# Two DRAM stretches with 64 KB rows in place of three stretches: x * y with a tanh GELU, one core

## The chip, the cores and the metric

One core of a Trainium2 chip. The time is the device time of one execution in microseconds (us); the kernel before takes 119.73 us (median of three runs, 119.72 to 119.74). Every later measurement has its own runs of the kernel before beside it on the same chip. A run would count as slow if it were over 1.5% above the fastest of its kernel. A **ratio** below is the mean time of one kernel's fast runs over the mean of the other's fast runs of the same rounds, with a 95% interval; it is therefore not quite the ratio of the medians that stand beside it.

## The reference

```python
batch, dim = 1024, 4096            # x, y: float32, 16 MiB each
z = x * y
out = 0.5 * z * (1 + tanh(sqrt(2 / pi) * (z + 0.044715 * z**3)))
```

It is elementwise, so any cut of the flat array into rows for the 128 partitions will do, as long as x, y and out are cut alike. 33.55 MB are read and 16.78 MB written.

## The kernel before

Each partition holds all of its 32,768 columns of x (128 KB); y gets room for 20,440 columns and is brought in by three loads. DRAM is cut into three stretches, each contiguous, with rows of 5 KB, 64 KB and 60,416 bytes for each partition (the code is shortened):

```python
PIECES = [(0, 1280), (1280, 17664), (17664, 32768)]            # x loads, and how DRAM is cut
Y_LOADS = [(1280, 17664, 4056), (17664, 32768, 0), (0, 1280, 15104)]   # columns, place in ys
Y_FREE = [0, 3, 4]                                             # multiplies done before that y load
STEPS = [[4096] * 4, [2048] * 7 + [768], [1280]]
STORES = [(1280, 17664), (17664, 32768), (0, 1280)]

def columns(t, a, b):                     # DRAM rows of columns a:b, contiguous stretch by stretch
    flat = t.flatten_outer_dims().rearrange("r c -> (r c)")
    pa, pb = next(q for q in PIECES if q[0] <= a and b <= q[1])
    return flat[P * pa : P * pb].rearrange("(p c) -> p c", p=P)[:, a - pa : b - pa]

_hoist(nc, [load_x(0).ins, load_x(1).ins])       # ahead of the start barriers, on SP's queue
load_y(0)
load_x(2)
for i in range(1, len(Y_LOADS)):
    if Y_FREE[i]:
        nc.sync.wait_ge(sem_mul, Y_FREE[i])
    load_y(i)
# ... for each load and each step of it: VectorE multiplies, ScalarE applies GELU, both in place in xs
for i, (a, b) in enumerate(STORES):
    if i == 0:
        nc.sync.wait_ge(sem_y[-2], 16)           # the second y load has landed
    nc.sync.wait_ge(sem_act, done[b])
    nc.sync.dma_start(out=columns(out, a, b), in_=xs[:, a:b]).then_inc(sem_o[i], 16)
```

All nine transfers go through one queue, in the order x (5 KB), x (64 KB), y (64 KB), x (60,416), y (60,416), y (5 KB), then the stores (64 KB, 60,416, 5 KB). Each of the 16 DMA engines moves eight rows of every transfer, one packet a row, with one ending packet of 4 bytes behind them: 16 x 9 x (8 + 1) = 1296 packets, as the trace has.

## Time and profile before

| | before |
|---|---|
| time, median | 119.73 us |
| span of the profiled run | 118.3 us |
| VectorE / ScalarE busy | 35.2 / 31.0 us |
| packets of the one queue | 1296, 98.8% of 16 engines' span |
| all loads landed (last 5 KB y packets) | 78.82 to 79.17 us |
| first store done, by engine | 98.30 to 98.49 us |
| second store issued | 96.33 us |
| last packet | 117.93 us |

The last four rows come from the trace's record of packets and instructions. (In the views DVE is VectorE, ACT is ScalarE, and SP is the engine that issues the transfers; an engine with a q, as SPq, is its sequencer.) To read it: the packets of the trace before move at 27.1 bytes per ns and engine for rows of 64 KB and of 60,416 bytes (medians 2420 and 2229 ns) and at 26.1 for rows of 5 KB (196 ns), so while every engine's packets follow without a gap, its time here goes with its bytes; what matters are the places where a transfer could reach an engine too late, and packets that take longer than others of their size.

### The profile page before, as it was taken

Reading aid. Unit: us, or ns where it says so; the run is one execution under the profiler, and the core shown is the slowest. Engines: PE = TensorE matmul, PEld = TensorE weight load, DVE = VectorE, ACT = ScalarE, POOL = GpSimd, SP = SyncE. Lnnn points to the kernel's source line nnn. Section 1 sums busy time; section 2 is a strip of 40 time slices with the busy share of each in tenths; the row PEclk is TensorE's granted clock in tenths of the full one; section 3 lists DMA queues with packets and bytes.
Section 4 is the critical chain, followed back from the end, with each engine's and each line's share of the span. In section 5 each row is a group of like instructions: output and inputs, shape, how many; then the busy total and the mean of one; then the engine's idle time right before and its main releaser. Section 6 shows DMA issues by size and latency. Waiting matters only on the chain.

```text
span 118.3 us, 82 instructions
## 1 busy us (share of the span) xinstructions
DVE 35.2 (30%) x13; ACT 31.0 (26%) x14; POOL 0.2 (0%) x4
## 2 busy tenths in 40 slices
DVE  0000000000000069999920000059999940000000
ACT  3000000000000001977974000007998990000000
POOL 0000000000000000000000000000000000000000
DMA  9988899889988897797797797798899888977975
GB/s 375 556 355 355 355 643 421 355 355 421 643 355 355 355 654 327 327 654 327 327 654 327 327 654 327 327 576 355 355 576 487 355 355 368 613 327 327 654 327 222
DMA packets 1296, 50.33 MB, mean 425 GB/s; under 512 B 144, under 2 KB 144, under 8 KB 528
## 3 DMA queue, kind: packets, MB, share of 16 engines
q1 hardware_dynamic: 1296, 50.33, 98.8%
HBM read 33.55 MB, written 16.78 MB: 425 GB/s over the span
## 4 chain that ended last, share of the span: by engine, by line
DMA 53%; DVE 24%; ACT 3%; issue 1%; DVEq 0%
DMA ys<-in_y_dram 53%; DVE xs L96 24%; ACT xs L104 3%; DVEq L93 0%
## 5 line engine op out<-in xcount | busy, mean ns | idle before, releaser
L96 DVE TENSOR_TENSOR xs<-xs,ys 128x2048 f32<-128x2048 f32 (+3 forms) x13 | 35.2, 2778 | 60.7 <-DMA ys<-in_y_dram 60.7
L104 ACT ACTIVATE xs<-xs 128x2048 f32<-128x2048 f32 (+3 forms) x13 | 29.7, 2301 | 64.5 <-DVE xs L96 64.5
L104 ACT ACT_TABLE_LOAD x1 | 1.3, 1283 | 1.9 <-PEq L59 1.9
L134 POOL MEMSET const-bfloat16-1.0<- 128x1 bf16 x1 | 0.1, 102 | 0.0
L134 POOL MEMSET const-uint8-127<- 128x1 uint8 x1 | 0.1, 102 | 0.0
L134 POOL MEMSET const-float32-0.0<- 128x1 f32 x1 | 0.1, 99 | 0.2 <-issue 0.2
L134 POOL MEMSET const-float32-1.0<- 128x1 f32 x1 | 0.1, 99 | 0.0
## 6 DMA issues: line engine op xcount, KB each, us to landing
xs<-in_x_dram SPq DMA_DIRECT2D x1, 7552.0 KB, 57.9
ys<-in_y_dram SPq DMA_DIRECT2D x1, 7552.0 KB, 22.5
out_dram<-xs SPq DMA_DIRECT2D x1, 7552.0 KB, 20.4
xs<-in_x_dram SPq DMA_DIRECT2D x1, 640.0 KB, 3.6
ys<-in_y_dram SPq DMA_DIRECT2D x1, 640.0 KB, 19.7
out_dram<-xs SPq DMA_DIRECT2D x1, 640.0 KB, 20.8
xs<-in_x_dram SPq DMA_DIRECT2D x1, 22.6
ys<-in_y_dram SPq DMA_DIRECT2D x1, 40.4
```

The costliest lines, as they stand in the source:

```text
L96: nc.vector.tensor_mul(out=xs[:, c : c + w], in0=xs[:, c : c + w], in1=ys[:, r + c - a : r + c - a + w],).then_inc(sem_mul, 1)
L104: nc.scalar.activation(out=xs[:, c : c + w], in_=xs[:, c : c + w], func=GELU).then_inc(sem_act, 1)
L134: nc = _bacc.Bacc("TRN2", target_bir_lowering=False, num_devices=1)
```

## The change

Two stretches with 64 KB rows. The 5 KB that are first of x and last of y become the tail of the second stretch's rows, so that one store of full 64 KB rows replaces the stores of 60,416-byte and 5 KB rows. Since that store needs the tail's columns as well, their step moves from the end to the second place.

```diff
@@ -11,14 +11,20 @@
 
 
 
-PIECES = [(0, 1280), (1280, 17664), (17664, 32768)]
+PIECES = [(0, 16384), (16384, 32768)]
+X_LOADS = [(31488, 32768), (0, 16384), (16384, 31488)]
 
-Y_LOADS = [(1280, 17664, 4056), (17664, 32768, 0), (0, 1280, 15104)]
+Y_LOADS = [(0, 16384, 4056), (16384, 31488, 0), (31488, 32768, 15104)]
 
 Y_FREE = [0, 3, 4]
 
-STEPS = [[4096] * 4, [2048] * 7 + [768], [1280]]
-STORES = [(1280, 17664), (17664, 32768), (0, 1280)]
+STEPS = [
+    *((0, c, 4096) for c in range(0, 16384, 4096)),
+    (1, 16384, 2048),
+    (2, 31488, 1280),
+    *((1, c, min(2048, 31488 - c)) for c in range(18432, 31488, 2048)),
+]
+STORES = PIECES
 Y_BUF = 20440
 
 
@@ -60,14 +66,14 @@
 
     xs = nc.alloc_sbuf_tensor("xs", [P, PIECES[-1][1]], F32).ap()
     ys = nc.alloc_sbuf_tensor("ys", [P, Y_BUF], F32).ap()
-    sem_x = [nc.alloc_semaphore(f"sem_x{i}") for i in range(len(PIECES))]
+    sem_x = [nc.alloc_semaphore(f"sem_x{i}") for i in range(len(X_LOADS))]
     sem_y = [nc.alloc_semaphore(f"sem_y{i}") for i in range(len(Y_LOADS))]
     sem_mul = nc.alloc_semaphore("sem_mul")
     sem_act = nc.alloc_semaphore("sem_act")
     sem_o = [nc.alloc_semaphore(f"sem_o{i}") for i in range(len(STORES))]
 
     def load_x(i):
-        a, b = PIECES[i]
+        a, b = X_LOADS[i]
         return nc.sync.dma_start(out=xs[:, a:b], in_=columns(x, a, b)).then_inc(sem_x[i], 16)
 
     def load_y(i):
@@ -84,32 +90,27 @@
             nc.sync.wait_ge(sem_mul, Y_FREE[i])
         load_y(i)
 
-    n = 0
-    done = {}
-    for i, (a, b, r) in enumerate(Y_LOADS):
-        for j, (xa, xb) in enumerate(PIECES):
-            if xa <= a < xb:
-                nc.vector.wait_ge(sem_x[j], 16)
-        nc.vector.wait_ge(sem_y[i], 16)
-        c = a
-        for w in STEPS[i]:
-            nc.vector.tensor_mul(
-                out=xs[:, c : c + w],
-                in0=xs[:, c : c + w],
-                in1=ys[:, r + c - a : r + c - a + w],
-            ).then_inc(sem_mul, 1)
-            n += 1
-            done[c + w] = n
-            nc.scalar.wait_ge(sem_mul, n)
-            nc.scalar.activation(
-                out=xs[:, c : c + w], in_=xs[:, c : c + w], func=GELU
-            ).then_inc(sem_act, 1)
-            c += w
+    seen = set()
+    for n, (i, c, w) in enumerate(STEPS, 1):
+        a, b, r = Y_LOADS[i]
+        if i not in seen:
+            seen.add(i)
+            nc.vector.wait_ge(sem_x[X_LOADS.index((a, b))], 16)
+            nc.vector.wait_ge(sem_y[i], 16)
+        nc.vector.tensor_mul(
+            out=xs[:, c : c + w],
+            in0=xs[:, c : c + w],
+            in1=ys[:, r + c - a : r + c - a + w],
+        ).then_inc(sem_mul, 1)
+        nc.scalar.wait_ge(sem_mul, n)
+        nc.scalar.activation(
+            out=xs[:, c : c + w], in_=xs[:, c : c + w], func=GELU
+        ).then_inc(sem_act, 1)
 
     for i, (a, b) in enumerate(STORES):
         if i == 0:
             nc.sync.wait_ge(sem_y[-2], 16)
-        nc.sync.wait_ge(sem_act, done[b])
+        nc.sync.wait_ge(sem_act, max(n for n, (_, c, _) in enumerate(STEPS, 1) if a <= c < b))
         nc.sync.dma_start(out=columns(out, a, b), in_=xs[:, a:b]).then_inc(sem_o[i], 16)
     for i in range(len(STORES) - 1):
         nc.sync.wait_ge(sem_o[i], 16)
```

## The prediction

Where the recorded texts are marked as cut, here and among the experiments, they said of the hardware what no trace or run of this case shows.

> **What bounds the kernel now.** I began with the page: the span, the busy times and the row of DMA shares.
>
> ```profile
> span 118.3 us, 82 instructions
> DVE 35.2 (30%) x13; ACT 31.0 (26%) x14; POOL 0.2 (0%) x4
> DMA  9988899889988897797797797798899888977975
> q1 hardware_dynamic: 1296, 50.33, 98.8%
> ```
>
> Both compute engines are idle for two thirds of the span, while the packets of one queue fill 98.8% of the 16 DMA engines' time. The dips in the DMA digits are not idle time: a packet of up to 64 KB is booked where it ends or starts, which is also why the GB/s row swings between 327 and 654. So the second thing I read was the trace's record of every DMA packet (start, length, size). Counting only the 1152 data packets: the first starts at 1.04 us, the last ends at 117.92 us, and in between all 16 engines have a packet in flight except in the first and last fraction of a microsecond. There are 384 packets each of 65,536, 60,416 and 5,120 bytes, with medians of 2420, 2229 and 196 ns. That is 27.1, 27.1 and 26.1 bytes per ns for one engine: a 5 KB row is only 4% less efficient than a 64 KB row. The other 144 packets carry 4 bytes, 9 ns each: one for each engine at the end of each of the nine transfers.
>
> The page's chain of waits gives 53% to the y loads and 24% to VectorE, and ends in ScalarE; it does not follow the queue, and here that matters. The waits of the DMA-issuing engine show the end better:
>
> ```profile
> SPq L115 <- DMA out_dram<-xs: 18.9, 1, 18.9
> SPq L113 <- ACT xs L104: 18.7, 2, 17.9
> SPq L113 <- DMA ys<-in_y_dram: 14.5, 1, 14.5
> SPq L119 <- SPq L119: 1.4, 1, 1.4
> ```
>
> The two waits on ScalarE (18.7 us together) are those ahead of the second and third store. [...]The timeline at that place tells how close it is:
>
> ```profile
> 93.66 3.80 ACT L104 ACTIVATE xs<-xs 128x2048 f32<-128x2048 f32 x3 [0.29 <-DVE xs L96]
> 94.41 1.49 DVE L96 TENSOR_TENSOR xs<-xs,ys 128x1280 f32<-128x1280 f32 x1
> 96.33 1.49 SPq L113 DMA_DIRECT2D out_dram<-xs  x2
> ```
>
> The second store is issued at 96.33 us, when the 768-column activation is done; the third at 97.49 us, when the 1280-column one is done. The packet records say that the engines finish the first store between 98.30 and 98.49 us. So the second store has 2.0 us to spare, and the third, queued behind 18 us of the second, has 18 us.
>
> [...]16 engines at 27.1 bytes per ns are 433 here[...]. The change gives the 5 KB transfers a pitch of 64 KB; [...]the 64 KB rows already lie at that pitch, and move at the same 27.1 as the 60,416-byte rows.[...]
>
> **The loads.** The same six transfers of the same row sizes are issued in the same order under the same waits; only where the 5 KB and 60,416-byte rows lie in DRAM changes. Packets before and after: 24 small, 24 of 60,416 and 24 of 65,536 bytes for each engine become 16, 16 and 32. I take 0 for the loads, with 0 to 0.2 us for the first transfer: its first packets now take 194 to 732 ns[...], and 128 rows spread over 8 MB could be colder than 640 KB in one piece.
>
> **The stores.** For each engine eight rows of 60,416 and eight of 5,120 bytes become eight of 65,536. Packets of one size follow each other a few ns sooner than their length, so by lengths: before, 8 x (2229 + 200) = 19,432 ns (the 5 KB store packets average about 200) plus one 9 ns semaphore packet more; after, 8 x 2418 = 19,344 ns. That saves about 0.09 us, 0.1 with the semaphore. One store issue (0.33 us) also goes, but it ran beside the stream and bounded nothing. So the whole of the intended gain is about 0.1 us, 0.1%.
>
> **What the order of the steps does.** The second store now needs all thirteen activations, not twelve. VectorE's total is unchanged: it starts at 78.12, and the 1280 step moves from last to second place. Its y has landed by then (the y wait passed at 79.62, and the second multiply starts at 80.33), so no new wait. From the rows by form, and the start of each instruction in the trace:
>
> ```profile
> L96 DVE TENSOR_TENSOR xs<-xs,ys 128x2048 f32<-128x2048 f32 x7 | 15.5, 2286 | 18.2 <-DMA ys<-in_y_dram 18.2
> ...
> L96 DVE TENSOR_TENSOR xs<-xs,ys 128x1280 f32<-128x1280 f32 x1 | 1.5, 1486 | 0.0
> ...
> L96 DVE TENSOR_TENSOR xs<-xs,ys 128x768 f32<-128x768 f32 x1 | 1.0, 951 | 0.0
> ```
>
> The 768 multiply starts at 93.54 before; with the 1280 step ahead of it, 1.49 - 0.08 = 1.40 us later, at 94.95. The last 2048 multiply therefore ends at 95.03. Its activation starts about 0.03 us later and takes 1.91 us: done at 96.97. The 768 activation overlaps it by 0.09 us and takes 0.83: done at 97.70. SP issues 0.025 us after an activation, as at 96.33 and 97.49: the second store goes out at about **97.73 us**, 1.40 us later than before, since a 768 step of ScalarE behind a 2048 step now closes the line.
>
> **What that does to the queue.** How soon does a store move data after its issue? The first store gives it: issued at 78.043, and four engines that had finished the last y packets early started its first packets at 78.887, 78.899, 78.920 and 78.951, waiting some 50 to 65 ns for them. So the earliest engine needs 0.84 us, and the sixteenth not more than 1.13 (it started at 79.178, when its own y work ended). Applied to 97.73 this gives first packets between 98.57 and at most 98.87. The engines are free at 98.30 to 98.50. So there is a **bubble of about 0.3 us** that the kernel before does not have, since its second store has a 2 us margin.
>
> **The sum.** The last engine starts at about 98.72 (between 98.62 and 98.87), moves 8 x 2415 = 19,320 ns by the pitch of packets, with 0.03 for the somewhat slower first ones and the semaphore: the last packet at about 98.72 + 19.35 = 118.07, against 117.93. The wait at the end passes 0.36 us after it, as now (118.287 against 117.926). Span about 118.45, so +0.15; I add 0.05 for the colder first load. Time: 119.73 + 0.2 = **119.93 us**, +0.17%: gain 0.1, bubble -0.3, load -0.05 or so, rounded.
>
> **The rivals.**
> 1. *The stream is what counts, and the bubble does not appear.* Fewer packets and stores then give about -0.1 us: 119.6. For it: the stream fills 98.8%. Against it: the margin of the second store sinks from 2.0 us to about 0.6, less than the 0.84 us that an issue takes. It would need ScalarE or VectorE 0.3 us faster than their rows.
> 2. *The 64 KB pitch slows the small loads.* [...]if a 5 KB packet took twice as long, two loads of eight packets for each engine would add 2 x 8 x 0.196 = 3.1 us: 122.9, slower by 2.6%. A fifth more would add 0.6. [...]Against: the 64 KB rows of this trace lie at this pitch, are walked by the engines nearly in step, and lose nothing.
> 3. *The 5 KB y load is late for its new place.* It is now needed second, not last. It lands at 79.18 and the wait passes at 79.62, while VectorE is busy until 80.4: 0.7 us of slack. If rival 2 held, this slack would go first, and each further delay would push the second store by as much, to the bubble's account.
>
> **Range and chances.** The bubble's size is set by two differences of a few tenths (97.73 and 0.84 to 1.13 against 98.30 to 98.50), and each can be off by 0.1 to 0.15; the cold load by 0.1; another chip by some hundredths. So 119.7 to 120.25 should hold it 8 times in 10. A gain of 2% would need 2.4 us, more than all idle time in the queue: chance 0.005. A loss of 2% needs rival 2 nearly in full: 0.03. Within 2%: 0.965.
>
> **What would show it.** Right, if the profile after has 1280 packets; two stores, the second issued near 97.7; a gap of 0.2 to 0.5 us at each DMA engine between the stores, where the kernel before has none; the loads' end still near 79.2. Wrong, if the 5 KB packets exceed 196 ns in the second small load, if the second store is issued before 97.4, or if its first packets follow the first store's without a gap.

## More of the kernel before

The page's list of transfers gives for each kind the KB and the us from issue to landing:

```profile
out_dram<-xs SPq DMA_DIRECT2D x1, 7552.0 KB, 20.4
xs<-in_x_dram SPq DMA_DIRECT2D x1, 640.0 KB, 3.6
ys<-in_y_dram SPq DMA_DIRECT2D x1, 640.0 KB, 19.7
out_dram<-xs SPq DMA_DIRECT2D x1, 640.0 KB, 20.8
```

The three small transfers (640 KB) take most of that time waiting in the queue (eight packets of 196 to 199 ns on average are 1.6 us for an engine, of 19.7 and 20.8), except the first x load, which nothing precedes: 3.6 us for 640 KB.

## The result, and the profile after

The changed kernel takes **120.44 us** (median of six runs, 120.38 to 120.69) against 119.75 (119.72 to 119.93): ratio 1.0061 [1.0048, 1.0074]. It is 0.6% slower, within the 2% that counts as the same, but above the range that was forecast. Measured once more, beside other runs of the kernel before: 120.58 against 119.81, ratio 1.0056 [1.0041, 1.0071].

First the page of the changed kernel: span, busy times, DMA shares, queue.

```profile
span 119.1 us, 80 instructions
DVE 35.2 (30%) x13; ACT 31.0 (26%) x14; POOL 0.2 (0%) x4
DMA  6998899888988898797797797798899888988888
q1 hardware_dynamic: 1152, 50.33, 98.6%
```

Compute is the same to a tenth. The queue has 1152 packets, 144 fewer. (The prediction's last paragraph said 1280: it took off the 16 ending packets of the store that goes and forgot its 128 rows, though its own count of 64 row packets for each engine, with one ending packet for each of eight transfers, gives 16 x 72 = 1152.) Next the waits of the DMA-issuing engine, the four longest, and the timeline around the issue of the second store:

```profile
SPq L81 <- DVE xs L100: 57.3, 2, 53.4
SPq L120 <- SPq L120: 19.5, 1, 19.5
SPq L114 <- ACT xs L106: 19.3, 1, 19.3
SPq L114 <- DMA ys<-in_y_dram: 14.5, 1, 14.5
```

```profile
93.42 1.91 ACT L106 ACTIVATE xs<-xs 128x2048 f32<-128x2048 f32 x1 [0.29 <-DVE xs L100]
95.62 2.64 ACT L106 ACTIVATE xs<-xs 128x2048 f32<-128x2048 f32 x2 [0.29 <-DVE xs L100]
98.28 0.34 SPq L114 DMA_DIRECT2D out_dram<-xs  x1
```

The first line is the wait for room in y, ahead of the later y loads. There is one wait of a store on ScalarE in line 114, where the kernel before had two in its line 113; the pair of activations that starts at 95.62 (2048 and 768 columns) ends at 98.26, and the store goes out at 98.28. Before, it was 96.33. Third, the rows of the multiplies by form, and the list of transfers:

```profile
L100 DVE TENSOR_TENSOR xs<-xs,ys 128x2048 f32<-128x2048 f32 x7 | 15.6, 2284 | 18.3 <-DMA ys<-in_y_dram 18.3
...
L100 DVE TENSOR_TENSOR xs<-xs,ys 128x1280 f32<-128x1280 f32 x1 | 1.5, 1485 | 0.0
...
L100 DVE TENSOR_TENSOR xs<-xs,ys 128x768 f32<-128x768 f32 x1 | 0.9, 949 | 0.0
```

```profile
xs<-in_x_dram SPq DMA_DIRECT2D x1, 640.0 KB, 4.2
ys<-in_y_dram SPq DMA_DIRECT2D x1, 640.0 KB, 19.7
out_dram<-xs SPq DMA_DIRECT2D x2, 20.8
```

The steps are as long as before. The first x load took 4.2 us where it took 3.6; the small y load, in the middle of the stream, is unchanged at 19.7.

The packet records say where 0.75 us of the profiled stream went (last packet at 118.67 us, against 117.93):

| from the packet records | before | after |
|---|---|---|
| first x load, 5 KB packets: longest | 732 ns | 1165 ns |
| first x load: landed, last engine | 3.20 us | 3.83 us |
| third x load: excess of its packets, per engine | 0.02 us | 0.17 us |
| all loads landed, last engine | 79.17 us | 79.68 us |
| first store done, mean of the engines | 98.38 us | 98.91 us |
| gap of an engine between first and second store, mean | 0.006 us | 0.274 us |
| first store done to last store done, means | 19.42 us | 19.67 us |

**Excess** here and below is the sum, over a transfer's packets, of the time beyond what packets of that size usually take (196, 2229 and 2418 ns), divided by 16 engines: roughly what a transfer loses per engine. The **gap** counts from the start of an engine's last ending packet, which takes 9 ns in the traces, so 0.006 us means no pause. So 0.5 us were lost by the end of the loads and 0.25 us in the stage of the stores.

### The profile page after: what moved, and what is told of

Read it like the earlier page. It is cut to its first block, busy times and chain, and to the rows that moved or that the text cites. A ratio compares the mean times of both kernels' runs of the same rounds, so it can differ in the third digit from the quotient of the medians.

```text
span 119.1 us, 80 instructions
## 1 busy us (share of the span) xinstructions
DVE 35.2 (30%) x13; ACT 31.0 (26%) x14; POOL 0.2 (0%) x4
## 2 busy tenths in 40 slices
DMA packets 1152, 50.33 MB, mean 423 GB/s; under 512 B 128, under 2 KB 128, under 8 KB 384
## 3 DMA queue, kind: packets, MB, share of 16 engines
q1 hardware_dynamic: 1152, 50.33, 98.6%
## 4 chain that ended last, share of the span: by engine, by line
DMA 53%; DVE 25%; ACT 2%; issue 1%; DVEq 0%
DMA ys<-in_y_dram 53%; DVE xs L100 25%; ACT xs L106 2%; DVEq L99 0%
## 6 DMA issues: line engine op xcount, KB each, us to landing
ys<-in_y_dram SPq DMA_DIRECT2D x1, 640.0 KB, 19.7
```

## The experiments

Theories at the outset. **T1:** the bubble between the stores costs about 0.3 us. **T2:** the first load is slow because its 128 short rows now lie spread over DRAM, and that costs the rest. Rivals: the gap or the slow first load cost nothing by themselves; it is the power-of-two pitch and not the spread; it is the new loop. Some kernels read wrong addresses on purpose, so their results are wrong in the columns concerned; this is said at each. Loads only read x, so such a probe moves the same bytes.

### First group, on one chip (119.80 us for the kernel before)

**e1_early_store**: the changed kernel with its last steps cut small, so that less of ScalarE's work stands behind VectorE's last multiply.

```diff
-    *((1, c, min(2048, 31488 - c)) for c in range(18432, 31488, 2048)),
+    # (1, start, columns), contiguous from 18432 on, of these sizes:
+    # 2048, 2048, 2048, 1536, 1536, 1280, 1024, 768, 768
```

> Only the step sizes at the end differ from the changed kernel: 1536, 1536, 1280, 1024, 768, 768 in place of three steps of 2048 and one of 768. From the rows of the changed kernel (VectorE 1.04 ns a column plus 71 ns a step, ScalarE 0.83 ns a column plus about 100 ns a step) the last activation should end at 97.46 us instead of 98.26, so the second store goes out 0.8 us earlier and its packets are ready before the engines finish the first store (98.84 to 99.01). Theory (the loss is 0.5 us of slow first load plus a bubble of about 0.25 us between the stores): the bubble goes, the rest stays: about 0.25 us faster than the changed kernel's 120.44, so 120.15 to 120.25, and no gap between the stores in the packet records. Rival (the first load alone made the loss, a gap between the stores is just how two stores of 64 KB rows follow each other): still 120.4.

Measured: 120.03 us, ratio 1.0030 [1.0014, 1.0046], against 1.0056 and 1.0061 for the changed kernel. Its timeline before the second store:

```profile
95.44 0.95 DVE L108 TENSOR_TENSOR xs<-xs,ys 128x768 f32<-128x768 f32 x1
95.67 1.59 ACT L114 ACTIVATE xs<-xs 128x768 f32<-128x768 f32 x2
97.29 0.34 SPq L122 DMA_DIRECT2D out_dram<-xs  x1
```

The store goes out at 97.29 us in place of 98.28, and every engine starts its packets 6 ns after the start of its last ending packet: the gap is gone, and with it 0.31 to 0.37 us (1.0056 to 1.0061 less 1.0030 is 0.26 to 0.31% of 119.8; each ratio is uncertain by about 0.2 us, so the packet records are the sharper evidence: 19.34 us from the first store's end to the last's in place of 19.67). That is T1, and about half of the loss. The other half stays.

**e2_contiguous** and **e3_pitch59k**: the changed kernel, its first load reading another part of x on purpose: 640 KB in one piece from the middle of x, or rows 60,416 bytes apart.

```diff
+        if i == 0:   # e2; wrong numbers on purpose
+            src = flat[P * 16384 : P * 16384 + P * 1280].rearrange("(p c) -> p c", p=P)[:, :1280]
+        if i == 0:   # e3; wrong numbers on purpose
+            src = flat[P * 16384 : P * 16384 + P * 15104].rearrange("(p c) -> p c", p=P)[:, :1280]
```

> The changed kernel, but the first small load reads its 128 rows of 5 KB from one contiguous stretch of 640 KB in x (wrong numbers in those 1280 columns on purpose). Theory (rows spread over 8 MB make the first packets slow): the first load's last packet ends near 3.2 us as before the change instead of 3.83, everything behind moves up by about 0.5 us, time about 119.95. Rival (the start of the changed kernel is slower for another reason, such as the instruction's form or the place in the tensor's second half): no change, 120.4.

> As the contiguous probe (wrong on purpose in those 1280 columns), but the 128 rows of 5 KB lie 60,416 bytes apart, over 7.7 MB, so not at a power of two. If it is the spread over many places not touched before, nothing comes back: first load done near 3.8 us, 120.4. If it is the power-of-two pitch[...], it is as the contiguous probe: done near 3.2 us, 119.95.

Measured: e2 120.36 us, ratio 1.0046 [1.0034, 1.0058]; e3 120.22 us, 1.0038 [1.0025, 1.0051]. Neither came out as one of its alternatives in full: in e2 the load landed as early as T2 said but the time was the rival's, and e3 lies between its two. In e2 the first load did land early (last engine 3.08 us, excess 0.20), but the long rows of the next loads were slower (excess 0.25 for the second x load and 0.18 for the first y load, against 0.02 and 0.01 in the changed kernel), and the total hardly moved. In e3 the first load has an excess of 0.50, less than the 0.78 of the changed kernel, so a power of two is not needed for a slow first load. Neither the clean T2 nor the pitch rival stands after this pair; it took the mirror experiments below, in a kernel without bubble.

**e4_long_first**: the changed kernel, the 64 KB rows of x loaded first.

```diff
-X_LOADS = [(31488, 32768), (0, 16384), (16384, 31488)]
+X_LOADS = [(0, 16384), (31488, 32768), (16384, 31488)]
```

> The changed kernel with the first two x loads in the other order: the 64 KB rows first, the 5 KB rows of x behind them. If the slow packets belong to the start (each engine's first reads are late, whatever is read), the 64 KB rows take the delay: first packets some 0.3 to 0.9 us over 2420 ns, and the 5 KB packets behind them 196 ns each; the end of the x loads near 22.9 us or a little less, time 120.2 to 120.4. If they belong to the 5 KB rows at their pitch, these are slow in second place too, and the long rows lose 0.1 us or so: 5 KB packets well over 196 ns, time 120.4. If a long first packet hides the delay of the reads behind it, up to 0.5 us comes back: 119.95.

Measured: 120.42 us, ratio 1.0051 [1.0039, 1.0063], about as the changed kernel. The long first packets now take up to 3238 ns (excess 0.64 us), and the same 5 KB rows in second place 202 ns on average. So in this run it is not the short rows at their pitch that are slow but the load that is read first.

### Second group: one part alone, in the kernel before (119.76 us for it)

**g1_before_spread**: the kernel before, its first load reading 5 KB rows 64 KB apart.

```diff
+        if i == 0:   # wrong numbers on purpose
+            src = flat[P * 16384 : P * 32768].rearrange("(p c) -> p c", p=P)[:, 15104:]
```

> The kernel before, only that its first small x load reads 128 rows of 5 KB that lie 64 KB apart, as the changed kernel's does (wrong numbers in those 1280 columns on purpose). So far a contiguous first load in the changed kernel gave 0.2 us of excess packet time per engine instead of 0.5 to 0.78, but the total hardly moved. Theory (spread rows cost at the start and this costs time): first load done at 3.5 to 3.8 us instead of 3.20, time 0.3 to 0.5 us over the kernel before: 120.1 to 120.3. Rival (what the spread first load loses, the long rows behind it win back, as the kernel before pays 0.18 us there): 119.8 to 119.9.

Measured: 120.05 us, ratio 1.0020 [1.0006, 1.0033], some 0.24 us. Its first small load takes nearly as long as in the changed kernel (KB, us from issue to landing):

```profile
xs<-in_x_dram SPq DMA_DIRECT2D x1, 640.0 KB, 4.1
```

The excess is 0.69 us in the first load, and 0.01 in the second, which costs 0.18 in the kernel before. So part of what the slow first load loses is won back at once, as the rival said, but a part of 0.24 us stays (0.07 to 0.40 us by the interval).

**g2_before_order**: the kernel before with the changed order of steps (and the changed kernel's loop for it), layout and stores as they were.

```diff
-STEPS = [[4096] * 4, [2048] * 7 + [768], [1280]]
+STEPS = [
+    *((0, c, 4096) for c in range(1280, 17664, 4096)),
+    (1, 17664, 2048),
+    (2, 0, 1280),
+    *((1, c, min(2048, 32768 - c)) for c in range(19712, 32768, 2048)),
+]
```

> The kernel before, only that the 1280-column step comes second in the last stretch and the 768-column step last, as in the changed kernel; layout, loads and three stores as before. Theory of the bubble: the second store is issued at 97.7 instead of 96.33 us, its packets start 0.2 to 0.3 us after the engines are free, time 0.2 to 0.3 us over the kernel before: 119.95 to 120.1. Rival (the gap costs nothing by itself): 119.8.

Measured: 120.09 us, ratio 1.0026 [1.0014, 1.0039], 0.31 us.

```profile
95.38 2.64 ACT L108 ACTIVATE xs<-xs 128x2048 f32<-128x2048 f32 x2 [0.29 <-DVE xs L101]
98.05 0.82 SPq L116 DMA_DIRECT2D out_dram<-xs  x2
```

The second store is issued at 98.05 in place of 96.33; the engines are free from 98.59 to 98.85 on, and get its packets after a mean gap of 0.273 us. From the first store's end to the last's it takes 19.75 us in place of 19.42. The bubble is shown from both sides: taken out of the changed kernel and put into the kernel before, 0.33 us each time in this stage.

**f3_three_pieces** and **h1_warm**: the early-store version, once with the tail as a third contiguous stretch at the end of DRAM with its own store (first line), once with a tiny load ahead of all (the rest).

```diff
+PIECES = [(0, 16384), (16384, 31488), (31488, 32768)]     # f3
+    warm = nc.sync.dma_start(                             # h1
+        out=ys[:, 0:128], in_=flat[: P * 128].rearrange("(p c) -> p c", p=P)
+    ).then_inc(sem_w, 16)
+    _hoist(nc, [warm.ins, load_x(0).ins, load_x(1).ins])
```

> The changed kernel with the early second store (smaller last steps, 120.03 in its own run), and the 5 KB columns as a third contiguous stretch at the end of DRAM with a store of their own, so long rows of 60,416 bytes are contiguous again and the first load is too. If the whole loss lies in the spread small rows and the bubble, this is level with the kernel before: 119.75 to 119.85. If the place (end of the tensor in place of its start) or the code of the loop matters, it stays at 120.0.

> The early-store version of the changed kernel (120.03 in its own run) with one more load ahead of all: 128 rows of 512 bytes, contiguous, into a part of the y buffer not yet in use. If the slow first packets are the engines' own start (any first read), the tiny load takes the delay and the 5 KB rows behind it move at 196 ns: first small load's excess under 0.1 us per engine, total 119.8 or less. If it is the spread of the rows over DRAM, the 5 KB packets are still slow behind the tiny load (excess 0.4 us or more) and the total is 120.0 to 120.2.

Measured: f3 120.04 us, ratio 1.0020 [1.0007, 1.0032], not level with the kernel before; its first load is contiguous but at another place, and has an excess of 0.41 us. h1 121.32 us, ratio 1.0124 [1.0111, 1.0138]: the 5 KB rows behind the tiny load are as slow as without it (excess 0.75 us), and start 0.5 us later. This first read of something else (128 rows of 512 bytes) did not help them (the runs without it have 0.62 to 0.78 us). That h1 is slower than e1_early_store by more than this later start is taken up with the tables.

### Third group: the control, the place, the other load (119.81 us for the kernel before)

**after_again** is the changed kernel unaltered.

> The changed kernel unaltered, once more, beside the kernel before on the chip of the other three runs of this call. Expected from its first measurement: 120.4 to 120.5, 0.6 to 0.7 us over the kernel before. If that came out at 0.55 (the bubble's 0.31 and the spread small load's 0.24 by the ratios of their own runs), nothing more would be left to explain; if at 0.7, some 0.15 us is.

Measured: 120.58 us, ratio 1.0056 [1.0041, 1.0071], so 0.67 us remained to be explained.

**i1_before_small_steps**: as g2_before_order, but the last steps 2048, 2048, 2048, 1536, 1536, 1280, 1024, 768, 768.

> The kernel before with the layout, loads and three stores as they were, but with the loop's order of the changed kernel (1280 columns second) and its last steps cut small as in the early-store version, so the second store is early. A control: in the early-store versions 0.24 to 0.36 us over the kernel before were left. If the smaller steps or the order cost something in themselves, this is at 119.9 or more; if not, at 119.7 to 119.8.

Measured: 119.86 us, ratio 0.9997 [0.9980, 1.0013]. The loop, the order and two more instructions on each engine cost nothing that shows (at most 0.16 us by the interval); what g2 lost was the late issue.

**i2_before_end** and **i3_before_x1_pitch**: the kernel before, its first load from a contiguous 640 KB at the end of x; or its third x load at a pitch of 64 KB.

```diff
+        if i == 0:   # i2; wrong numbers on purpose
+            src = flat[P * 31488 : P * 32768].rearrange("(p c) -> p c", p=P)
+        if i == 2:   # i3; wrong numbers on purpose
+            src = flat[P * 16384 : P * 32768].rearrange("(p c) -> p c", p=P)[:, :15104]
```

> The kernel before, only that its first small x load reads a contiguous 640 KB from the end of x in place of the start (wrong numbers in 1280 columns on purpose). The version with three contiguous stretches (5 KB columns at the end of DRAM) had no bubble and no spread rows and was still 0.24 us (0.07 to 0.32%) over the kernel before. If the place far from the next load's rows is what costs, this is at 119.95 to 120.05; if place does not matter, at 119.75 to 119.8.

> The kernel before, only that the third x load reads its rows of 60,416 bytes at a pitch of 64 KB as in the changed kernel (wrong numbers in those columns on purpose). In the changed kernel and three of its variants two waves of this load's packets were 100 to 200 ns slow, 0.16 to 0.27 us per engine; in the kernel before they were not. If that comes from the pitch: 0.15 to 0.25 us slower, 119.9 to 120.0, with slow packets near 46 to 49 us. If it comes and goes by itself: 119.75.

Measured: i2 120.09 us, ratio 1.0017 [1.0000, 1.0034], excess of the first load 0.50 us, though it is in one piece. i3 119.96 us, ratio 1.0013 [0.9996, 1.0030], about 0.16 us, but with an interval that includes no loss at all; its third load has an excess of 0.26 us, from the third and fourth packets of most engines, as in the changed kernel's first profile (in its second, the first four packets).

### Fourth group: what is special in the third load, and what is left of the gain (119.75 us for the kernel before)

**j1_x1_pitch60k** and **j2_x1_place**: as i3, at a pitch of 60 KB, and contiguous from the same start.

```diff
+            src = flat[P * 16384 : P * 31744].rearrange("(p c) -> p c", p=P)[:, :15104]   # j1, wrong on purpose
+            src = flat[P * 16384 : P * 31488].rearrange("(p c) -> p c", p=P)              # j2, wrong on purpose
```

> The kernel before, the third x load reading rows of 60,416 bytes at a pitch of 60 KB (61,440 bytes), from the same start as in the 64 KB pitch run (wrong numbers in those columns on purpose). If the power of two[...], the two slow waves vanish: third load's excess per engine under 0.06 us, time 119.75 to 119.8. If any gap between rows does it, excess 0.15 to 0.27 us and 119.95.

> The kernel before, the third x load contiguous as it was but starting at the middle of x, where the 64 KB pitch run started, instead of 640 KB further on (wrong on purpose). If the place makes the slow waves, they are here: excess 0.15 to 0.27 us, 119.95. If the pitch does, none: under 0.06 us, 119.75 to 119.8.

Measured: j1 119.82 us, ratio 1.0005 [0.9992, 1.0018], excess of the third load 0.04; j2 119.81 us, ratio 1.0001 [0.9989, 1.0013], excess 0.02. In the packet records neither the place (0.02) nor the gaps (0.04) bring the slow packets, and the 64 KB pitch does (0.26 in i3). What they cost in time is not shown: by time alone i3 and these two are not told apart, since the intervals overlap.

**j3_one_store_only**: the early-store version, all x loads from the addresses of the kernel before (wrong on purpose).

```diff
+            src = flat[: P * 1280].rearrange("(p c) -> p c", p=P)                  # i == 0
+            src = flat[P * 1280 : P * 17664].rearrange("(p c) -> p c", p=P)        # i == 1
+            src = flat[P * 17664 :].rearrange("(p c) -> p c", p=P)                 # i == 2
```

> The early-store version of the changed kernel, its three x loads reading the addresses of the kernel before (wrong on purpose): what is left of the change is the second store of 64 KB rows in place of two, and the y loads at their new addresses. If bubble, spread first load and the third load's pitch are the whole loss, the merged store's gain of 0.05 to 0.1 us stands alone: 119.65 to 119.75. If the y loads lose something as well, 119.85 or more.

Measured: 120.14 us (119.72 to 120.38), ratio 1.0027 [1.0013, 1.0042]: a miss. The second y load, which lies at the 64 KB pitch too, now has the slow packets (excess 0.21 us, against 0.005 in the changed kernel). A loss had moved from x to y. From the first store's end to the last's it took 19.35 us, 0.05 to 0.08 less than the kernels with three stores.

**j4_two_x_loads**: a correct version, early store and x in two loads of 64 KB rows.

```diff
-X_LOADS = [(31488, 32768), (0, 16384), (16384, 31488)]
+X_LOADS = [(0, 16384), (16384, 32768)]
```

> A correct version of the new layout: early second store, and x in two transfers of 64 KB rows in place of three, so there is neither a spread small load nor a third load with gaps. The first packets are then the cold ones of the long rows (excess 0.64 us per engine in the run with the long rows first, against 0.42 us for the first two loads of the kernel before). Expected 119.9 to 120.0: better than the changed kernel by 0.5, a little behind the kernel before. If the long first rows hide the cold start, 119.7.

Measured: 120.26 us, ratio 1.0039 [1.0027, 1.0051], above the 119.9 to 120.0 expected. The long first packets are slow (up to 3481 ns, excess 0.74 us), and the second y load has the slow packets (0.18). By ratio it lies between the changed kernel and e1_early_store, with intervals that overlap. No version beat the kernel before; the control i1 is level with it.

### The packet records of all runs side by side

Store stage, mean landing of the first store to mean landing of the last, in us:

| kernels | gap between the stores | stage |
|---|---|---|
| three stores, early: before, f3, g1, i1, i2, i3, j1, j2 | 0.006 | 19.40 to 19.43 |
| three stores, late issue: g2 | 0.273 | 19.75 |
| two stores, late issue: after (twice), e2, e3, e4 | 0.24 to 0.28 | 19.64 to 19.68 |
| two stores, early: e1, h1, j3, j4 | 0.006 | 19.34 to 19.35 |

Excess of the loads, us per engine:

| what the load reads | excess |
|---|---|
| first load, 5 KB rows, contiguous from the start of x (before, g2, i1, i3, j1, j2, j3) | 0.19 to 0.36 |
| the same from the middle of x (e2) | 0.20 |
| the same from the end of x (f3, i2) | 0.41, 0.50 |
| 5 KB rows 60,416 bytes apart (e3) | 0.50 |
| 5 KB rows 64 KB apart, first of the program's large loads (after twice, e1, g1, h1) | 0.62 to 0.78 |
| 5 KB rows 64 KB apart, in mid-stream (y, after) | 0.002 |
| 60,416-byte rows contiguous or 60 KB apart, third x load (before, f3, g1, g2, i1, i2, j1, j2, j3) | 0.01 to 0.12 |
| 60,416-byte rows 64 KB apart, the first such load of a kernel (after twice, e1, e2, e3, h1, i3, j3, j4) | 0.14 to 0.41 |
| the same in e4 | 0.01 |
| the second such load of a kernel (y: after twice, e1, e2, e3, e4, h1) | 0.005 to 0.03 |

One more place where the queue runs dry is in these records. An engine waits between its last y packet and its first packet of the first store, counted like the gap, on average 0.02 us in the kernel before, 0.03 and 0.12 us in the two profiles of the changed kernel, 0.17 us in g1, 0.16 us in i2 and 0.39 us in h1. The first store is issued only when the long y rows have landed on every engine; at that moment the first and the last engine are 0.35 us apart in the kernel before, 0.60 in g1 and 0.91 in h1, and an engine that is far ahead finishes its last eight small packets before the store can begin (in the trace before the first engine is done at 78.83 us, and the store's first packet starts at 78.887). So part of g1's 0.24 us, and 0.34 us of what h1 loses against e1_early_store, arises there and not in the first load itself. No experiment changed this alone.

## Why the prediction was wrong

**The direction and the bubble were right.** The prediction put the second store's issue at 97.73 us, with the loads where they were. The trace after has 98.285, and VectorE's first multiply of that stretch starts at 78.679 in place of 78.120, 0.56 us later; 98.285 - 0.56 is 97.73. It put first packets 0.84 to 1.13 us after the issue; they came after 0.84 to 0.99 us (99.124 to 99.275). It put the bubble at about 0.3 us; the gap is 0.274 us, taking it away won 0.31 to 0.37 us and putting it into the kernel before cost 0.31 us.

**The gain of the merged store was right.** Forecast 0.09 us; the store stage without a bubble takes 19.34 to 19.35 us with two stores and 19.40 to 19.43 with three: 0.05 to 0.09 us.

**Rival 1 is refuted**: the bubble did appear. **Rival 3 did not happen**: the small y load took 19.7 us in both, and the wait for it passed at 80.19 us while the multiply ahead of it ran to 80.97.

**The step that failed is "The loads": "I take 0 for the loads, with 0 to 0.2 us for the first transfer"**, entered into the sum as 0.05. In the trace after, the loads end 0.5 us later and VectorE's last stretch starts 0.56 us later. Two terms were too small. The first transfer alone costs 0.24 us (g1). And the third load, taken as 0 because "the 64 KB rows already lie at that pitch, and move at the same 27.1", has an excess of 0.14 to 0.41 us per engine (0.16 us of time by i3's point estimate, whose interval includes 0): full 64 KB rows at that pitch do move at 27.1 bytes per ns (median 2420 ns), but in the first load of 60,416-byte rows at it two waves or more of packets are slow (not in e4, 0.01 us), and packets of the same size 60 KB apart are not (0.04 us, j1). The prediction's rival 2 named the pitch, but looked for it in the 5 KB packets, which stay at 196 ns in mid-stream, and set it aside on the evidence of the full rows. That the forecast was right about the bubble is no luck: issue, first packets and gap each came out as worked.

**The sum with measured terms**: bubble 0.31 (g2), merged store -0.08 (stage times), first load 0.24 (g1), third load 0.16 (i3): 0.63 us, against 0.67 to 0.73 measured by the two ratios. Each term from a ratio is uncertain by 0.16 to 0.2 us, so the sum closes within what was measured, no better; a missing or a spurious term of 0.2 us would not show in it.

**What stays open.** Why the first reads are slow is not shown; the prediction's "cold" is a name for it, not a cause. Short rows spread over 8 MB lose 0.62 to 0.78 us per engine as the first load, but one piece at the end of x loses 0.50 (i2) and one piece in the middle 0.20 (e2); a tiny load ahead did not help (0.75, h1). "Spread" is what the changed kernel does, not a mechanism. Why only the first load with 60,416-byte rows at 64 KB suffers, and why e4 escapes, is open too; and in j3 the slow y packets and the store's gain sum to 0.13 us (0.21 - 0.08), less than the 0.32 us measured; in its trace the engines also wait 0.10 us ahead of the first store, against 0.02 before, which leaves about 0.1 us.

## What to carry to other kernels

Here one queue was full from start to end (98.8% of 16 engines' span), and fewer and longer transfers, issued in time, gained only what their packets saved, 0.05 to 0.09 us in the stage of the stores (19.34 to 19.35 against 19.40 to 19.43). In such a case ask first whether the new transfer can be issued before the queue runs dry, with the issue-to-first-packet time of that same trace (0.84 to 0.99 us here) as the margin to keep. When a merge makes a transfer wait for more work, try ending that work on small steps (here the store went out at 97.29 us in place of 98.28, and 0.31 to 0.37 us came back). And do not take a change of DRAM addresses as free because sizes and order stay (new addresses for the first load alone cost 0.24 us in g1): compare packet times of the same kind of rows, in the same place in the stream, before calling it 0.
